# Splitting 45 of the second layer's weights ahead of time into memory, and moving one PSUM bank from dense to small products

## The chip, the cores and the metric

The kernel runs on one core of a Trainium2 chip. The metric is the device time of one execution in microseconds (us), the median of three runs for the kernel before. TensorE is called PE below, VectorE DVE, ScalarE ACT, GpSimd POOL, and SyncE, which here does nothing but issue the DMAs, SP.

## The reference, cut to what matters

Two layers over 512 positions of width 1024, float32, and a final norm:

```
h = x + even_layer(rms_norm(x, g0), w_in (1024 x 7168), ..., w_out (2048 x 1024))
h = h + odd_layer(rms_norm(h, g1), w_in (1024 x 5248), ..., w_out (1536 x 1024))
out = rms_norm(h, final_norm_g)

even_layer: p = h @ w_in, split in 7; a gated width-3 convolution and a gated
            128x128 position mixing; concat @ w_out
odd_layer:  p = h @ w_in, split in r, k, v, two low-rank streams, gate zc, fd, zd;
            RWKV-7 scans forward and backward, 16 heads of 64; a 2-D DFT branch on fd;
            SiLU gates; concat @ w_out
```

## The kernel before, in words

**Dense products.** A weight is cut into pieces of 128x1024 (512 KB): 8 (`pv`), 48 (`ub`, `zb`, `xa`, `ca`, `za`, `ba`) and 16 (`e0_*`, `e1_*`, the output projection) in the first layer, 41 input blocks (`wa`, `k`, `r`, `v`, `zc`, `fd`, `zd`) and 12 output pieces (`o0_*`, `o1_*`) in the second. PE multiplies in float32r, so each piece is split first: hi = the piece copied to float32r, lo = piece - hi, and likewise the activations; a product is the three matmuls hi*hi, hi*lo, lo*hi (`mm3`). One input block is 24 matmuls of 512 columns into one PSUM bank. So a weight costs one DMA (`loads`, tile `wf_...` of ring `wq`), one cast (`copy`: ACT, or DVE where the planner finds that sooner) and one subtraction (`less`: POOL or DVE, likewise) in `splits`.

**Small products.** The scans are cut into chunks of 64 positions. For each of 8 pairs of heads j there are many small float32 matmuls: scores (`sm`, `sa`, `sz`), a 64x64 triangular inverse by blocks (`iH`, `iTT`, `iTB`, `iG`, `iTJ`, with a long row of small DVE operations `iA`, `iT` ahead of it), `sp`, `sg`, and the chain over 8 chunks (`pa`, `py`, DVE's `X`). Each result in PSUM goes to SBUF by a DVE or ACT operation before its bank is free.

**Order.** Every part is a generator, a *strand* with a rank. `Plan.run` builds the program in one pass: it picks, time after time, the operation that could start first by the planner's own table of costs (lower rank first among equals) and appends it to its engine's queue. The engines then run these queues in order. A tile is taken from a ring of fixed size (`get`) and given back (`free`); a strand that finds no free tile waits. Rings that matter here: `wq` (5 tiles of 512 KB), `kb` (2), `a` (2), `zg` (3) of 256 KB; and the PSUM rings `d` (3 banks: dense blocks, the low-rank products `zw`, `za`, and `bo`) and `s` (3 banks: the small products, most of which ask for two banks at once), `py`, `pa` (1 each). At most 3 weights are loaded and not yet split (`credit`).

Of the kernel before, what the change touches and what calls it, by code (L numbers as in the profile page):

```python
# [12 lines left out]
F32 = mybir.dt.float32  # L13
# [11 lines left out]
C = 64  # L25
# [392 lines left out]
OUTS = 0, 1, 2, 4, 5, 3  # L418
LAST = 1, 2
FLAGS = False, False, False  # L420


class Slabs:
# [9 lines left out]
class K:  # L433
# [42 lines left out]
    def turned(self, x, s, h, g, key, ss):  # L476
# [14 lines left out]
        self.free("zg", t)  # L491
        self.plan.done.add(f"{key}{s}_{h}")

    def loads(self):
        yield "go"
        for i, (key, src, shape) in enumerate(self.weights):
            if key == "wa0":
                for _ in range(2):
                    yield from self.plan.credit("load", 3)
            yield from self.plan.credit("load", 3)  # L500
            wf = self.wf[key] = yield from self.get("wq", f"wf_{key}", shape)
            yield self.Q.dma_start(wf, src)
            self.plan.done.add(f"wf_{key}")

    def splits(self):

        layer0 = True
        for i, (key, src, shape) in enumerate(self.weights):
            layer0 = layer0 and key != "wa0"
            yield f"wf_{key}"  # L510
            if key == "pv1_0":
# [2 lines left out]
            if key.startswith("pv") and key.endswith("_0"):  # L514
                at = []
                for tag in ("G", "ops"):
                    at.append((tag, (yield from self.get(tag, f"w{tag}_{key}", shape, F32R))))
                tiles = [t for _, t in at]
            elif key in (f"o0_{OUTS[-1]}", f"o1_{OUTS[-2]}"):
                at = []  # L520
                for n in "hl":
                    at.append(("xw", (yield from self.get("xw", f"w{n}_{key}", dt=F32R))))
                tiles = [t for _, t in at]
            elif key in ("e1_5", "e1_6"):
                tag, low = ("wq", "k") if key == "e1_5" else ("E", "r")
                t = yield from self.get(tag, f"w_{key}", shape, F32R)
                at = [(tag, t)]
                for _ in range(2):
                    at.append((low, (yield from self.get(low, f"w_{key}", [P, 1, 512], F32R))))
                tiles, parts = [t, Slabs(at[1][1], at[2][1])], [slice(0, 1), slice(1, 2)]  # L530
            elif key == "e1_7":
                at = []
                for tag in ("a", "a", "w", "w"):
                    at.append((tag, (yield from self.get(tag, f"w_{key}", [P, 1, 512], F32R))))
                tiles, parts = [Slabs(at[0][1], at[1][1]), Slabs(at[2][1], at[3][1])], [slice(0, 1), slice(1, 2)]
            else:
                low = "hi" if key == "k0" else "wq" if not layer0 else "xw" if key[0] in "puz" and key[:2] != "za" else ("hi", "E")[i % 2]
                tiles, at = [], []
                for tag in ("wq", low):
                    t = yield from self.get(tag, f"w_{key}", shape, F32R)  # L540
                    tiles.append(t)
                    at.append((tag, t))
# [22 lines left out]
    def project(self, name, n, y, res, pair):  # L565

        for d in range(2):
            ps, tags = [None] * NS, (("d", "d", "d", "py"), ("s", "s", "s", "d"))[d]
            for bs in [(b,) for b in range(n - 3)] + ([(n - 3, n - 2, n - 1)] if d == 1 and pair else [(n - 3,), (n - 2,), (n - 1,)]):
                for b in bs:  # L570
                    yield f"w_{name}{d}_{b}"
# [970 lines left out]
    def project_o(self, d):  # L1542
# [5 lines left out]
        else:  # L1548
            self.gb = yield from self.get("vq", "fin_gb", [P, D])
            yield self.Q.dma_start(self.gb, self.I["fin_g"].to_broadcast([P, D]))  # L1550
        ps, tags = [None] * NS, (("d", "d", "d", "s"), ("pa", "s", "s", "py"))[d]
        def part(b, s):
            w = self.w[f"o{d}_{b}"][0]
            if ps[s] is None:
# [82 lines left out]
    def run(self):  # L1637
        I = self.I
        with ExitStack() as ctx:
# [2 lines left out]
            self.tp = tp = self.pool(ctx, "work")  # L1642
            self.ip = self.pool(ctx, "scan")
            dram = self.pool(ctx, "dram", 1, bass.MemoryType.DRAM)
            dp, sp, yp, cp = (self.pool(ctx, name, n, PSUM) for name, n in (("dense", 3), ("short", 3), ("outs", 1), ("chain", 1)))
            self.h1 = dram.tile([S, D], F32, name="h1_dram")
            self.yd = dram.tile([6, P, S], F32, name="y_dram")
            fz = dram.tile([8, P, S], F32, name="f_dram")
# [13 lines left out]
                self.ring(tag, shape, 1, self.ip)  # L1662
            self.ring("X", [P, 4, 64], 2, self.ip)
            self.ring("wq", [P, KB, P], 5, self.wp)
            self.ring("d", [P, S], 3, dp)
            self.ring("s", [P, 8, C], 3, sp)
            self.ring("py", [P, S], 1, yp)
            self.ring("pa", [P, 4, 64], 1, cp)
            self.blocks = [("wa", 0), ("k", 0)] + list(FIRST)
# [15 lines left out]
            at = {"wa": 24, "k": 8, "r": 0, "v": 16, "zc": 25, "fd": 33, "zd": 37}  # L1685
            self.weights += [(f"{b}{j}", I["w_o"][at[b] + j], [P, KB, P]) for b, j in self.blocks]
            self.weights += [(f"o{d}_{b}", I["w_oo"][d, b], [P, 2, 512]) for d in range(2) for b in OUTS]
            self.w, self.wf, self.out, self.g = {}, {}, {}, [{"j": j} for j in range(8)]
            self.yh0, self.yl0, self.fss, self.h2 = {}, {}, {}, [None] * NS
            self.pool_r, self.pool_k, self.pool_t = FLAGS  # L1690
            for rank, gen in ((0, self.chain()), (1, self.start()), (1, self.build()), (3, self.post()), (4, self.loads()), (4, self.splits()), (4, self.prep()),
                              (5, self.products()), (6, self.params1()), (6, self.unit_states()), (FR, self.fnet()), (6, self.reload())):
                plan.strand(rank, gen, rank == 0, rank == 5)
            plan.run()
# [26 lines left out]
```

## Time and profile before

| what | value |
|---|---|
| median of 3 runs | 1087.21 us (1084.24 to 1088.44) |
| profiled execution | 1090.07 us, span 1088.3 us |
| instructions in the span | 27301 |
| busy: PE, DVE, ACT, POOL | 94%, 60%, 43%, 11% |
| DMA | 91.51 MB, 84 GB/s over the span |
| granted PE clock, mean | 0.983 |

"Busy" counts the time in which an engine had at least one instruction running; PE's matmuls are pipelined and their records overlap. The span goes from the first to the last instruction. All operations are recorded in one place, line 401, so tiles, not lines, tell what an instruction is; buffer numbers are left out of names.

### The profile page before, as it was taken

To read this page: it belongs to the slowest core of one execution; us is meant where nothing else is said; L and a number is where in the kernel's file an instruction comes from. 1 tells how busy PE (TensorE), PEld (TensorE's weight loads), DVE (VectorE), ACT (ScalarE), POOL (GpSimd) and SP (SyncE) were. 2 spreads that over 40 slices of the span, in tenths; PEclk is the share of its full clock that TensorE was granted. 3 is DMA by queue.
4 is the path that set the end of the run, shared out by engine and by line. 5 is a ranking of instruction groups with operands and counts; after the bars stand their busy time and mean duration, and the time that the engine had idled before them with its cause. 6 is when DMAs were issued, how large, how long until landed. Compare 5 with 4: busy or idle time off the path is not lost. (4 is left out here: it accounts for less than half of the span.)

```text
span 1088.3 us, 27301 instructions
## 1 busy us (share of the span) xinstructions
PE 1024.3 (94%) x12024; PEld 839.3 (77%) x12024; DVE 651.3 (60%) x1225; ACT 472.7 (43%) x795; POOL 124.9 (11%) x155
## 2 busy tenths in 40 slices
PE   7999999999999999998898999989988899999997
PEld 6988888888888888876676778767767677777776
DVE  6464444344343336895795858867793976864453
ACT  7232222222222125753565455744644736453253
POOL 1001210010110010220012101321021201110000
PEclk9999999999999999999998999989998999999999
DMA  8322222322223332332012011110121111154033
GB/s 286 105 73 94 81 94 98 97 97 97 96 96 124 130 116 98 100 105 89 8 46 89 3 42 61 49 52 21 41 71 41 60 39 48 60 172 131 30 107 117
DMA packets 32663, 91.51 MB, mean 84 GB/s; under 512 B 4896, under 2 KB 7712, under 8 KB 32544
## 3 DMA queue, kind: packets, MB, share of 16 engines
q1 hardware_dynamic: 32544, 89.77, 25.1%
q8 instruction: 94, 1.54, 0.6%
q14 instruction: 25, 0.20, 0.1%
HBM read 81.82 MB, written 7.86 MB: 82 GB/s over the span
## 5 line engine op out<-in xcount | busy, mean ns | idle before, releaser
L401 PE MATMUL pe<-w_e,yh 128*128 128x512 f32 x256 | 81.5, 398 | 0.0
L401 PE MATMUL sg<-ops 64*128 64x128 f32 x512 | 66.6, 294 | 7.2 <-ACT am L401 2.1
L401 PEld LDWEIGHTS sg<-ops 64*128 64x128 f32 x512 | 53.9, 196 | 17.1 <-issue 3.9
L401 PE MATMUL sg<-pt,am 64*128 64x128 f32 x512 | 60.5, 283 | 0.0
L401 PEld LDWEIGHTS pe<-w_e,yh 128*128 128x128 f32 x256 | 48.1, 188 | 11.6
L401 ACT COPY gq<-sg 128x256 f32<-128x256 f32 x64 | 23.2, 370 | 71.7 <-DVE gq L401 70.5
L401 PEld LDWEIGHTS sg<-pt,am 64*128 64x128 f32 x512 | 52.3, 195 | 0.0
L401 PE MATMUL pd_zc<-hh,w_zc 128*128 128x512 f32 x128 | 50.5, 437 | 1.3 <-DVE w_zc L401 1.3
L401 PE MATMUL pe<-w_e,yl 128*128 128x512 f32 x128 | 50.3, 393 | 0.0
L401 DVE TENSOR_TENSOR w_e<-wf_e,w_e 128x1024 fp32r<-128x1024 f32 (+1 forms) x19 | 20.0, 1074 | 48.0 <-ACT w_e L401 47.8
L401 PE MATMUL pd_r<-hh,w_r 128*128 128x512 f32 x128 | 45.5, 409 | 2.0 <-DVE w_r L401 2.0
L401 DVE TENSOR_TENSOR gq<-sg,c_masks 128x256 f32<-128x256 f32 x64 | 25.6, 416 | 33.7 <-PE sg L401 33.7
L401 PE MATMUL pd_k<-hh,w_k 128*128 128x512 f32 (+1 forms) x144 | 44.6, 372 | 0.0
L401 PEld LDWEIGHTS pa<-X,gq 128*64 128x64 f32 x448 | 30.8, 139 | 17.1 <-issue 3.9
L401 ACT CAST w_e<-wf_e 128x1024 fp32r<-128x1024 f32 (+1 forms) x19 | 16.9, 913 | 62.4 <-PE pe L401 54.6
L401 PE MATMUL pd_v<-hh,w_v 128*128 128x512 f32 x128 | 43.8, 410 | 0.0
L401 PE MATMUL pa<-X,gq 128*64 128x64 f32 x448 | 38.8, 230 | 4.6 <-DVE X L401 2.0
L401 PE MATMUL pa<-c_cen,vq 128*64 128x128 f32 x256 | 42.6, 288 | 0.0
L401 PE MATMUL pd_ub<-hh,w_ub 128*128 128x512 f32 x128 | 40.5, 393 | 0.0
L401 PE MATMUL pd_zb<-hh,w_zb 128*128 128x512 f32 x128 | 40.4, 392 | 0.0
L401 PE MATMUL pd_xa<-hh,w_xa 128*128 128x512 f32 x128 | 40.4, 392 | 0.0
L401 PE MATMUL pd_ca<-hh,w_ca 128*128 128x512 f32 x128 | 40.4, 392 | 0.0
(362 smaller groups left out, 2831.4 us busy)
## 6 DMA issues: line engine op xcount, KB each, us to landing
wf_e<-in_w_eo SPq DMA_DIRECT2D x16, 512.0 KB
wf_o<-in_w_oo SPq DMA_DIRECT2D x12, 512.0 KB
wf_pv<-in_w_ev SPq DMA_DIRECT2D x8, 512.0 KB
wf_ub<-in_w_e SPq DMA_DIRECT2D x8, 512.0 KB
wf_zb<-in_w_e SPq DMA_DIRECT2D x8, 512.0 KB
wf_xa<-in_w_e SPq DMA_DIRECT2D x8, 512.0 KB
wf_ca<-in_w_e SPq DMA_DIRECT2D x8, 512.0 KB
wf_za<-in_w_e SPq DMA_DIRECT2D x8, 512.0 KB
```

The source lines that it names most:

```text
L401: i = op.call(*op.a, **op.kw)
```

## The change

Two edits, both in the code that makes the order. (1) A new strand of the lowest rank, `stash`, runs once the first norm is done. For the last 45 of the 53 weights of the second layer (33 input blocks, all 12 output pieces) it loads each in two halves of 256 KB, casts (`sh`), subtracts (`sl`; on POOL unless DVE would be done 4.0 us sooner by the planner's costs) and writes both results to a tensor in device memory, `w_dram`. `loads` then brings such a weight as two DMAs of 512 KB, hi and lo (`wh_...`, `wl_...`), and `splits` handles the other 80 alone. (2) The PSUM ring `d` has 2 banks in place of 3, `s` 4 in place of 3; three lists of tags follow.

```diff
+EARLY, STASH = 8, 4.0
+    def stash(self):
+        yield "consts"
+        yield "n0_3"
+        for n, (key, src, shape) in enumerate(self.late):
+            w = self.ws[key] = self.wd[n]
+            for i in range(2):
+                c = slice(4 * i, 4 * i + 4) if shape[1] == KB else slice(i, i + 1)
+                x = yield from self.get("zg", f"sf_{key}{i}")
+                yield self.Q.dma_start(x.rearrange("p (a b) -> p a b", b=shape[2]), src[:, c])
+                self.plan.done.add(f"sf{2 * n + i}")
+                self.plan.strand(7, self.apart0(2 * n + i, key, x, [w[h, :, i * S:i * S + S] for h in range(2)]))
+    def apart0(self, n, key, x, to):
...
+        hi = yield from self.get("kb", f"sh{n}", dt=F32R)
+        yield self.copy(hi, x)
+        lo = yield from self.get("a", f"sl{n}", dt=F32R)
+        yield self.less(lo, x, hi, STASH)
+        self.free("zg", x)
...
+        yield self.Q.dma_start(to[0], hi[:].bitcast(F32))
+        self.free("kb", hi)
+        yield self.Q.dma_start(to[1], lo[:].bitcast(F32))
+        self.free("a", lo)
     def loads(self):
...
+            if key in late:
...
+                for h in range(2):
+                    t = yield from self.get(tag, f"w{'hl'[h]}_{key}", shape, F32R)
+                    yield self.Q.dma_start(t[:].bitcast(F32).rearrange("p a b -> p (a b)"), self.ws[key][h])
     def project(self, name, n, y, res, pair):
-            ps, tags = [None] * NS, (("d", "d", "d", "py"), ("s", "s", "s", "d"))[d]
+            ps, tags = [None] * NS, (("d", "s", "s", "py"), ("s", "s", "d", "s"))[d]
     def project_o(self, d):
-        ps, tags = [None] * NS, (("d", "d", "d", "s"), ("pa", "s", "s", "py"))[d]
+        ps, tags = [None] * NS, (("d", "d", "s", "s"), ("pa", "s", "s", "py"))[d]
     def run(self):
-            dp, sp, yp, cp = (self.pool(ctx, name, n, PSUM) for name, n in (("dense", 3), ("short", 3), ("outs", 1), ("chain", 1)))
+            dp, sp, yp, cp = (self.pool(ctx, name, n, PSUM) for name, n in (("dense", 2), ("short", 4), ("outs", 1), ("chain", 1)))
-            self.ring("d", [P, S], 3, dp)
-            self.ring("s", [P, 8, C], 3, sp)
+            self.ring("d", [P, S], 2, dp)
+            self.ring("s", [P, 8, C], 4, sp)
+            self.late, self.ws = self.weights[-(len(self.blocks) - EARLY + 12):], {}
+            self.wd = dram.tile([len(self.late), 2, P, 1024], F32, name="w_dram")
```

Since the planner places everything anew, the order changes on all engines. On SP's queue, in the first layer's blocks, before the change there are only the weights of these blocks:

```order
L401 DMA wf_xa_1832<-in_w_e 128x1024
L401 DMA wf_xa_1868<-in_w_e 128x1024
L401 DMA wf_ca_1902<-in_w_e 128x1024
L401 DMA wf_ca_1937<-in_w_e 128x1024
L401 DMA wf_za_1971<-in_w_e 128x1024
L401 DMA wf_za_2006<-in_w_e 128x1024
```

On the same queue in the changed kernel, at the first `xa` weights (`sf` a half that is loaded, `sh` and `sl` its parts):

```order
L401 DMA wf_xa_1538<-in_w_e 128x1024
L401 DMA w_dram<-sh_1504 128x512
L401 DMA w_dram<-sl_1514 128x512
L401 DMA sf_r_1560<-in_w_o 128x512
L401 DMA w_dram<-sh_1532 128x512
L401 DMA w_dram<-sl_1543 128x512
L401 DMA sf_r_1582<-in_w_o 128x512
L401 DMA wf_xa_1599<-in_w_e 128x1024
L401 DMA sf_zd_1608<-in_w_o 128x512
L401 DMA w_dram<-sh_1566 128x512
L401 DMA w_dram<-sl_1575 128x512
```

Between two weights of the first layer there now stand five to six DMAs of 256 KB, two of three of them writes that wait for ACT's or POOL's result. All 270 of them (90 loads, 180 writes) stand between the sixth `pv` weight and the first `e` weight.

On PE's queue in the second layer, at the last chunks of the chain of the sixth pair of heads, before the change a dense block (`pd_zc`) and the product `bo` stand between two steps of the chain (`pa`, `py`):

```order
L401 MATMUL pa<-X_5_6556,gq_10_6484 64x64
L401 MATMUL py_6331<-gq_10_6484,X_5_6556 64x64 x4
L401 MATMUL bo_0_6572<-hi_0_6573,ones_193 128x512 x2
L401 MATMUL pd_zc_6206<-hh,w_zc_6193 128x512
L401 MATMUL pd_zc_6206<-hl,w_zc_6193 128x512
L401 MATMUL pd_zc_6206<-hh,w_zc_6194 128x512
```

At the same place on PE's queue of the changed kernel there are small products alone:

```order
L401 MATMUL pa<-X_5_7313,gq_10_7253 64x64
L401 MATMUL py_7125<-gq_10_7253,X_5_7313 64x64 x4
L401 MATMUL sz_10_7361<-ops_3931 64x128
L401 MATMUL sz_10_7361<-ops_3934 64x128
L401 MATMUL sz_11_7362<-ops_3931 64x128
L401 MATMUL sz_11_7362<-ops_3934 64x128
```

The dense blocks have moved together: the longest row of small products without a dense one between is 170 instructions before and 286 after, with the same matmuls in all.

## Rows read from the trace of the kernel before

**Rows 1.** The page: engines' busy time, and the span in 40 slices.

```profile
PE 1024.3 (94%) x12024; PEld 839.3 (77%) x12024; DVE 651.3 (60%) x1225; ACT 472.7 (43%) x795; POOL 124.9 (11%) x155
...
PE   7999999999999999998898999989988899999997
...
DVE  6464444344343336895795858867793976864453
```

**Rows 2.** Busy time by stage: stretch, length, engines busy, PEclk, DMA share, GB/s.

```profile
25.00:313.00 288.00, 288.00 (x1441) 244.09 (x1440) 132.00 (x177) 80.25 (x105) 26.14 (x23) 1.00 0.28 92
313.00:434.00 121.00, 121.00 (x572) 99.75 (x571) 47.11 (x62) 37.45 (x52) 10.49 (x13) 1.00 0.35 118
434.00:1043.00 609.00, 559.07 (x9744) 448.25 (x9743) 436.29 (x925) 320.75 (x575) 84.79 (x112) 0.97 0.19 62
```

**Rows 3.** Who waited for whom, PE alone, 434 to 1043 us.

```profile
PE iTT L401 <- DVE iHs L401: 7.5, 3, 3.3
PE iTB L401 <- issue: 3.3, 2, 2.2
PE iH L401 <- issue: 3.3, 2, 2.1
...
PE pd_r L401 <- DVE w_r L401: 2.0, 1, 2.0
...
PE pd_zc L401 <- DVE w_zc L401: 1.3, 2, 0.9
```

**Rows 4.** The chain that ended last: first and last of its six pieces on splits.

```profile
859.92 1.13 DVE w_k L401
...
1032.66 1.22 DVE w_o L401
```

**Rows 5.** Groups by shape from 400 us on: splits on DVE, ACT and POOL.

```profile
L401 DVE TENSOR_TENSOR w_k<-wf_k,w_k 128x1024 fp32r<-128x1024 f32 x8 | 9.8, 1226 | 0.6 <-ACT w_k L401 0.4 <-issue 0.2
...
L401 DVE CAST w_v<-wf_v 128x1024 fp32r<-128x1024 f32 x1 | 1.7, 1725 | 0.0
...
L401 DVE CAST w_k<-wf_k 128x1024 fp32r<-128x1024 f32 x1 | 0.7, 684 | 0.0
...
L401 ACT CAST w_k<-wf_k 128x1024 fp32r<-128x1024 f32 x7 | 7.3, 1049 | 3.6 <-DMA wf_k<-in_w_o 3.6
...
L401 ACT CAST w_e<-wf_e 128x512 fp32r<-128x512 f32 x6 | 3.2, 618 | 4.6 <-PE pe L401 4.6
...
L401 POOL TENSOR_TENSOR w_v<-wf_v,w_v 128x1024 fp32r<-128x1024 f32 x4 | 9.7, 2436 | 62.7 <-ACT w_v L401 40.5 <-PE pd_fd L401 14.5 <-PE iH L401 7.7
```

**Rows 6.** DMA share and rate (last two columns) in three short stretches.

```profile
5.00:10.00 5.00, 2.94 (x13) 2.47 (x14) 2.32 (x6) 4.71 (x10) 0.00 (x0) 1.00 1.01 391
10.00:15.00 5.00, 4.55 (x19) 3.67 (x17) 5.00 (x10) 5.00 (x10) 0.00 (x0) 1.00 1.06 367
966.00:970.00 4.00, 4.00 (x23) 3.30 (x21) 0.91 (x3) 3.34 (x4) 0.00 (x0) 1.00 0.94 293
```

**Rows 7.** SP's queue in order of time, first and last of six transfers of 256 KB.

```profile
963.42 0.94 SPq L401 DMA_DIRECT2D yf<-y_dram  x1
...
966.30 0.43 SPq L401 DMA_DIRECT2D xr<-h_dram  x1
```

**Rows 8.** Same, then ACT: a 512 KB load with nothing beside it.

```profile
402.57 0.33 SPq L401 DMA_DIRECT2D wf_wa<-in_w_o  x1
...
406.42 1.05 ACT L401 CAST w_wa<-wf_wa 128x1024 fp32r<-128x1024 f32 x1 [2.87 <-DMA wf_wa<-in_w_o]
```

**Rows 9.** SP and ACT in order of time: loads of two blocks, their casts.

```profile
86.82 6.77 SPq L401 DMA_DIRECT2D wf_ub<-in_w_e  x2
...
101.87 1.05 ACT L401 CAST w_ub<-wf_ub 128x1024 fp32r<-128x1024 f32 x1 [4.39 <-PE pd_zb L401]
```

**Rows 10.** By tile, PE: count, duration ns min/median/max, first and last start.

```profile
L401 PE MATMUL pd_ub<-hh,w_ub x128: 387/392/476, 61.5 to 143.8; 128*128 128x512 f32 x128
...
L401 PE MATMUL pe<-w_e,yh x256: 386/398/478, 332.6 to 423.7; 128*128 128x512 f32 x128
```

More of the change, by code (lines that the diff above doesn't have):

```diff
@@ L492, in turned @@
         self.plan.done.add(f"{key}{s}_{h}")
+    def stash(self):
[10 more added lines that the diff above has]
+    def apart0(self, n, key, x, to):
+        if n + 1 < 2 * len(self.late):
+            yield f"sf{n + 1}"
+        if n:
+            yield f"sl{n - 1}"
+        hi = yield from self.get("kb", f"sh{n}", dt=F32R)
+        yield self.copy(hi, x)
+        self.plan.done.add(f"sh{n}")
+        lo = yield from self.get("a", f"sl{n}", dt=F32R)
+        yield self.less(lo, x, hi, STASH)
+        self.free("zg", x)
+        self.plan.done.add(f"sl{n}")
+        if n + 1 < 2 * len(self.late):
+            yield f"sh{n + 1}"
+        yield self.Q.dma_start(to[0], hi[:].bitcast(F32))
+        self.free("kb", hi)
+        yield self.Q.dma_start(to[1], lo[:].bitcast(F32))
+        self.free("a", lo)
+        self.plan.done.add(f"st{n}_")
     def loads(self):
         yield "go"
+        late = {key for key, _, _ in self.late}
         for i, (key, src, shape) in enumerate(self.weights):
+            if key in late:
+                if key == self.late[0][0]:
+                    yield f"w_{self.weights[i - 1][0]}"
+                n = 2 * [k for k, _, _ in self.late].index(key)
+                yield f"st{n}_"
+                yield f"st{n + 1}_"
+                tag, at = "xw" if key in (f"o0_{OUTS[-1]}", f"o1_{OUTS[-2]}") else "wq", []
+                for h in range(2):
+                    t = yield from self.get(tag, f"w{'hl'[h]}_{key}", shape, F32R)
+                    yield self.Q.dma_start(t[:].bitcast(F32).rearrange("p a b -> p (a b)"), self.ws[key][h])
+                    at.append((tag, t))
+                self.w[key] = [t for _, t in at], at
+                self.plan.done.add(f"w_{key}")
+                continue
             if key == "wa0":
@@ L507, in splits @@
         layer0 = True
-        for i, (key, src, shape) in enumerate(self.weights):
+        for i, (key, src, shape) in enumerate(self.weights[:len(self.weights) - len(self.late)]):
             layer0 = layer0 and key != "wa0"
@@ L517, in splits @@
                     at.append((tag, (yield from self.get(tag, f"w{tag}_{key}", shape, F32R))))
[L518 to L522, printed above, removed]
                 tiles = [t for _, t in at]
@@ L1690, in run @@
             self.pool_r, self.pool_k, self.pool_t = FLAGS
-            for rank, gen in ((0, self.chain()), (1, self.start()), (1, self.build()), (3, self.post()), (4, self.loads()), (4, self.splits()), (4, self.prep()),
+            for rank, gen in ((0, self.chain()), (1, self.start()), (1, self.build()), (3, self.post()), (4, self.loads()), (4, self.splits()), (7, self.stash()), (4, self.prep()),
                               (5, self.products()), (6, self.params1()), (6, self.unit_states()), (FR, self.fnet()), (6, self.reload())):
```

## The prediction, made before the changed kernel was run

> **What bounds the kernel now.** I read the page first, then busy time by stage, then PE's waits, then the chain, then the DMA rows. The page shows PE busy 94% of the span, DVE 60%, and by slices two different halves: PE is full from the second slice to the seventeenth, while DVE stands at three or four tenths; after that PE loses a tenth in most slices and DVE stands at seven to nine [rows 1]. The stages say it in us. From 25 to 313 us (the first layer's blocks) PE is busy all 288 us, DVE 132, ACT 80, POOL 26, and the DMA engines 0.28 of their time. From 434 to 1043 us (the second layer up to the end of its small products) PE is busy 559 of 609 us, so 49.9 us are idle, with DVE at 436 (72%) and ACT at 321 (53%) [rows 2]. So the first layer is bound by PE alone, and its other engines have room. The second is PE too, but with 50 us of waits, and the most that any change to the other engines can give there is those 50 us and what the clock takes: a mean of 0.97 is 0.03 x 609 x 2 = 37 us at the lower level.
>
> Who ends these waits? By PE's own list about 9 us are "issue" (its instruction stream, which no other engine shortens; the two largest are 3.3 each), 2.0 + 1.3 = 3.3 us are a dense block waiting for DVE's subtraction for its weight, and some 36 us are small products waiting for DVE or ACT, the largest the inverse (`iTT`, 7.5) [rows 3]. The chain that ended last, which the trace follows back to 860 us, runs in turn over DVE and PE and has six pieces that are splits, 7.28 us in all (1.13, 1.05, 1.62, 1.21, 1.05, 1.22) out of 228 [rows 4].
>
> **What the change does, part by part.**
>
> *Second layer, splits gone.* Of the splits of the second layer the order shows 48 fewer on DVE (41 subtractions, 7 casts), 38 fewer casts on ACT, 4 fewer subtractions on POOL. At 1.226 us a subtraction and about 0.95 a cast (eight on DVE, from 0.684 to 1.725), DVE loses 50.3 + 6.7 = 57 us, and ACT 38 x 1.049 = 40 us [rows 5]. That is 13% of DVE's work in this stage and 12% of ACT's. What PE gets of it: the 3.3 us of direct waits go (a weight can now be late only by its DMA). Of the other 36 us, between nothing (each wait is a dependency that stands anyway) and all. I take a quarter, twice the share of the work that goes, since an in-order queue at 72% makes more than its share of lateness: 9 us. A check from the chain: 7.28 us in 228, taken over 654 us from 434 to the end, would be 21 us if nothing else became late in their place. My 12.3 us lies between the direct waits and that.
>
> *Second layer, DMA.* 45 weights cost two DMAs in place of one: 23.6 MB more over 609 us, 39 GB/s beside the 62 that are there at a share of 0.19. That is hidden. Its cover is the ring: two tiles for the block that runs, two for the next, one over. A load with nothing beside it took 3.85 us from issue to use [rows 8] and a block on PE lasts 5.65 us (48 blocks of 24 matmuls from 61.5 to 332.6 us [rows 10]), so it comes in time. If it were uncovered, each block would wait up to 3.85 us; I take nothing.
>
> *PSUM.* The fourth small bank lets the next pair of banks fill while the last is emptied; the second edit of the order shows what it costs: with two dense banks `pd`, `zw`, `za` and `bo` queue for the same two, dense blocks stand together, and small products run 286 instructions on end where it was 170. Where small products stand alone, PE can hide no wait. Both go into the quarter above; their bounds are 0 and the 36 us on one side, and on the other side a rival below. The clock I leave as it is: both signs are possible, with 37 us at the lower level to win from.
>
> *First layer, splits added.* 90 casts of 128x512: 86 on ACT by the order, at 0.618 us 53 us in 288 where ACT is busy 80; 90 subtractions on POOL at half of 2.436 us, 110 us where POOL is busy 26 [rows 2, 5]. Both fit. POOL and DVE can hold each other up (a DVE cast that takes 0.684 us elsewhere took 1.725 once [rows 5]): at worst 90 times 1.04 us, 94 us on a DVE with 156 us free. Cover enough; what would be late without it is emptying a dense bank, of which there are now two, one per 5.65 us of matmuls. The three tag lists give the output projections as many banks as before from other rings; PE is busy 121 of 121 us there [rows 2], and I take nothing.
>
> *First layer, DMA: the term that can turn the sign.* Between 25 and 313 us SP now issues 90 loads and 180 writes of 256 KB, 70.8 MB, beside 50 weights of 512 KB, 26.2 MB. 97.0 MB in 288 us is 337 GB/s, where it was 92 [rows 2]. What can the DMA engines do? With 512 KB loads queued they moved 391 and 367 GB/s at a share of 1.01 and 1.06 [rows 6]. With six transfers of 256 KB issued within 3.3 us [rows 7] the stretch 966 to 970 shows 293 GB/s at 0.94, so 312 at a full share [rows 6]. Mixed by bytes, with 379 as the mean of the first two, 70.8/312 + 26.2/379 = 227 + 69 = 296 us, 8 us more than there are. Slack: a weight was issued at 86.82 us and cast at 101.87, when ACT waited for PE and not for the load [rows 9]; less the 3.85 us of a load, 11 us of delay cost nothing. So the middle estimate costs 0, the lower rate as it stands (97.0/293 = 331 us, 43 - 11) costs 32, the higher rates cost 0. SP itself has time (320 issues at about 0.4 us in 288 us), but it waits in order: behind a write that waits for POOL stand the next weights of the first layer, and PE waits for those. I take 3 us for that.
>
> **Sum.** Against the profiled execution, 1090.07 us: -3.3 - 9 + 3 = -9.3 us, 1080.8 us. The runs' median is 2.9 us below that execution, so 1077.9; I say 1078 us, 0.85% faster.
>
> **The rivals.**
>
> *The first layer becomes bound by its DMAs (slower).* For it: 337 GB/s wanted, 293 to 312 seen with transfers of this size, and writes beside reads on queues that wait for two engines. Against it: 367 to 391 seen with a deep queue, and the order gives the weights a lead. At 293 GB/s: +32 - 12.3 = +20, 1107 us. The point from which it decides: it costs nothing down to 97.0/299 = 324 GB/s, and eats the whole gain of 12.3 us at 97.0/311 = 312.
>
> *The pieces do not overlap.* If every transfer paid its own latency in turn, as the lone load did (3.85 us for 512 KB [rows 8]; 0.69 less for 256 KB at 379 GB/s), 270 x 3.16 + 50 x 3.85 = 1046 us would stand in place of 288, and the whole would be some 1820 us. The six that were issued in 3.3 us and moved at 293 GB/s [rows 6, 7] speak against it. The Trainium skill, SBUF — State Buffer, section on the DMA setup-cost knee, measured 224 GB/s for single transfers of 256 KiB; by that the stage would be 97.0/224 = 433 us, an estimate of some 1210 us in all. The 293 GB/s of this trace is above that, because here several transfers were queued.
>
> *PE's waits only change their owner (no change).* With 94% busy and 9 us of issue, the inverse's row of DVE operations still stands ahead of `iTT`; the direct 3.3 us go and SP's 3 us come: 1087 us.
>
> *All of it is won.* The 36 us, the 3.3 and nothing lost: 1087.2 - 39 = 1048 us; for it speaks DVE's part in the chain, against it that waits on dependencies remain.
>
> *Dense blocks run out as cover.* If the longer rows of small products open new waits of 1 to 3 us at each of the eight pairs of heads, 8 to 24 us come back; with none of the quarter won, about 1100 us.
>
> **How the numbers follow.** This kernel's runs differ by 0.4%, so a change under 0.5% (5.4 us) can't be told from none. Forecast (a gain of 6 to 25 us): 0.40. All won or nearly: 0.12. Together faster 0.52. No change: 0.20. Slower: DMA-bound 0.20, dense cover 0.06, pieces that don't overlap 0.02, together 0.28. The likeliest case's own range is 1062 to 1081. The range of 8 in 10 runs from 1055 (it leaves out some 0.08 of "all won") to 1110 (it leaves out the pieces that don't overlap and DMA rates under 293, some 0.08).
>
> **What would show each step.** Right, if PE is still busy all through the blocks, the first `pe` matmul stays near 333 us, and the DMA share in the blocks is 0.85 to 0.98; wrong, if PE shows waits for `w_ub`, `w_xa` and their like and the first `pe` comes 10 us or more later: the DMA rival. In the second layer DVE's busy time should be down by some 50 us and PE's idle time in it from 50 us to about 38; if DVE is down and PE's idle time is not, the waits have changed owner; if new waits of `sg`, `sp`, `sa` for `gq`, `am`, `zz` come up inside long rows of small products, it is the dense cover. Waits of `pd` matmuls for DMAs of `wh` or `wl` would show that the reload is not hidden. The prediction fails most easily on the DMA rate with writes among reads, which no row of before shows at this load.

## The result, and the profile after

The changed kernel takes 1159.39 us, median of 4 runs (1158.99 to 1171.45), beside 1087.71 us of the kernel before (1084.24 to 1088.44, 4 runs): ratio 1.068, 95% interval 1.065 to 1.072, so 6.8% slower. The prediction said 1078 us, 1055 to 1110. The profiled execution took 1159.49 us where that of before took 1090.07: 69.4 us more, and three places of the trace say where. The page, busy time and the slices (PE, granted clock, DMA share, GB/s), answers to [rows 1]:

```profile
PE 1050.3 (91%) x12024; PEld 848.5 (73%) x12024; DVE 617.6 (53%) x1182; ACT 482.8 (42%) x842; POOL 234.9 (20%) x241
...
PE   7969888988798799999989999899998898999997
...
PEclk9979998999899899999999999999999999999999
DMA  8777778888787742332430232213150403335344
GB/s 299 262 238 250 234 263 275 264 284 273 235 262 248 261 128 91 129 126 93 154 139 8 96 123 84 80 56 114 43 168 9 156 8 115 116 130 176 117 155 163
```

The tiles `pe` and `pd_ub` (as [rows 10]) say when the first layer's blocks end and how long one matmul takes, the windows (as [rows 2], cut at the first `pe` and the first `pd_wa`, the start of the second layer) what the engines did:

```profile
L401 PE MATMUL pe<-w_e,yh x256: 387/398/477, 420.9 to 512.0; 128*128 128x512 f32 x128
...
L401 PE MATMUL pd_ub<-hh,w_ub x128: 387/394/793, 67.4 to 180.1; 128*128 128x512 f32 x128
```

```profile
25.00:421.00 396.00, 343.03 (x1524) 272.93 (x1523) 162.78 (x190) 129.46 (x195) 150.93 (x117) 0.93 0.76 251
421.00:512.00 91.00, 91.00 (x400) 73.33 (x399) 34.04 (x44) 26.71 (x36) 3.68 (x6) 1.00 0.37 125
512.00:1157.00 645.00, 598.76 (x9995) 486.18 (x9993) 404.76 (x919) 309.17 (x581) 78.53 (x112) 0.98 0.31 104
```

First layer: the first `pe` comes at 420.9 us in place of 332.6, 88.3 us late. Of these PE is idle 53 (396 less 343.0), and its 343 busy us hold the work that took 308 before (25 to 332.6): the other 35. The granted clock was 0.93 in place of 1.00, because in some stretches the lower of the two levels was granted (a `pd_ub` matmul takes up to 793 ns there, where 476 was the most before [rows 10]). That accounts for at most 0.07 x 396 = 28 of the 35 us; the rest was not followed. Output projection: 91.5 us as before. Second layer: from `pd_wa` to the end 645.3 us where it was 664.1, 18.8 us won. 88.3 - 18.8 - 0.1 = 69.4.

PE's own waits, first layer (top five) and second layer (top three, to set against [rows 3]):

```profile
PE pd_ub L401 <- DVE w_ub L401: 12.0, 4, 5.4
PE pd_ba L401 <- DVE w_ba L401: 6.7, 3, 3.1
PE pd_ca L401 <- ACT w_ca L401: 6.7, 3, 3.8
PE pv L401 <- ACT x L401: 4.2, 2, 4.0
PE pd_ba L401 <- ACT za L401: 3.9, 3, 1.6
...
PE iTB L401 <- issue: 6.8, 2, 3.5
PE sm L401 <- issue: 4.1, 4, 1.7
PE iH L401 <- issue: 3.6, 3, 2.0
```

In the first layer PE waits mostly for the splits of that layer's own weights (40 us by the whole list); the other 12 are dense banks that are emptied late (`x`, `za` and their like). Neither is ACT or DVE short of time (129 and 163 us busy of 396). What they and POOL wait for stands in the list of all engines for 25 to 421 us, and then in SP's:

```profile
ACT sh L401 <- DMA w_dram<-sh: 164.8, 61, 10.7
POOL sl L401 <- DMA w_dram<-sl: 80.6, 21, 6.3
POOL sl L401 <- ACT sh L401: 69.5, 24, 7.5
...
SPq L401 <- POOL sl L401: 167.5, 80, 4.9
```

ACT stands 165 us before casts of the stash, because by the profile the tile for the result is still being written out; behind that cast in ACT's queue stands `w_ca`, for which PE waits. SP stands 168 us for POOL's subtractions. The rows in order of time show how these close a ring (SP, then ACT, then POOL):

```profile
205.26 0.33 SPq L401 DMA_DIRECT2D sf_zc<-in_w_o  x1
205.65 0.42 SPq L401 DMA_DIRECT2D w_dram<-sh  x1
206.12 0.42 SPq L401 DMA_DIRECT2D w_dram<-sl  x1
207.77 0.33 SPq L401 DMA_DIRECT2D sf_k<-in_w_o  x1
208.15 0.44 SPq L401 DMA_DIRECT2D w_dram<-sh  x1
...
211.79 0.33 SPq L401 DMA_DIRECT2D sf_k<-in_w_o  x1
...
209.79 0.62 ACT L401 CAST sh<-sf_zc 128x512 fp32r<-128x512 f32 x1 [0.84 <-DMA w_dram<-sh]
...
212.26 0.62 ACT L401 CAST sh<-sf_zc 128x512 fp32r<-128x512 f32 x1 [0.42 <-DMA w_dram<-sh]
...
206.46 1.29 POOL L401 TENSOR_TENSOR sl<-sf_v,sh 128x512 fp32r<-128x512 f32 x1
210.49 1.27 POOL L401 TENSOR_TENSOR sl<-sf_zc,sh 128x512 fp32r<-128x512 f32 x1 [2.74 <-ACT sh L401]
```

The load at 207.77 goes out the moment a subtraction ends (206.46 + 1.29) and frees its source tile. The write at 205.65 lands, and 4.14 us after its issue the cast two pieces later can start (209.79); for the next write 4.11 (208.15 to 212.26). The subtraction follows (210.49 to 211.76), and at 211.79 SP's next load. Over all pieces the median from a write's issue to the cast that it holds up is 4.29 us, and a piece takes 4.15 us (first to last of 90 subtractions). The order has less room. At the last stash load, 387.9 us, PE had 33 us of blocks left; at full speed that load would stand 33 us before 332.6, so 90 loads lie between 21.4 and 300 us: 3.1 us each. Fixed orders turn the difference into a toll on PE: about 1 us for each of 90 pieces.

### The profile page after: what moved, and what is told of

Same layout as the page of the kernel before. It is cut to its first block, busy times and chain, and to the rows that moved or that the text cites. A ratio compares the mean times of both kernels' runs of the same rounds, so it can differ in the third digit from the quotient of the medians.

```text
span 1157.7 us, 27995 instructions
## 1 busy us (share of the span) xinstructions
PE 1050.3 (91%) x12024; PEld 848.5 (73%) x12024; DVE 617.6 (53%) x1182; ACT 482.8 (42%) x842; POOL 234.9 (20%) x241
## 4 chain that ended last, share of the span: by engine, by line
PE 50%; DVE 10%; issue 3%; ACT 3%; DMA 1%; SPq 0%; POOL 0%; DVEq 0%; ACTq 0%
PE pe L401 8%; PE po L401 6%; PE pd_zc L401 4%; PE pd_v L401 4%; PE sg L401 4%; PE pd_r L401 3%; PE pd_k L401 3%; DVE iA L401 2%; PE pd_fd L401 2%; PE pa L401 2%; DVE iT L401 2%; PE pd_zd L401 1%; PE sp L401 1%; DVE gq L401 1%; PE sm L401 1%
## 5 line engine op out<-in xcount | busy, mean ns | idle before, releaser
L401 PE MATMUL sg<-ops 64*128 64x128 f32 x512 | 61.9, 285 | 2.3 <-ACT pt L401 1.3
L401 PE MATMUL pd_ub<-hh,w_ub 128*128 128x512 f32 x128 | 46.2, 439 | 15.9 <-DVE w_ub L401 12.0
L401 PEld LDWEIGHTS sg<-ops 64*128 64x128 f32 x512 | 49.8, 187 | 9.0 <-ACT pt L401 2.9
L401 PE MATMUL pd_ba<-hh,w_ba 128*128 128x512 f32 x128 | 45.4, 430 | 10.8 <-DVE w_ba L401 6.7
L401 PE MATMUL pd_ca<-hh,w_ca 128*128 128x512 f32 x128 | 44.5, 424 | 8.3 <-ACT w_ca L401 6.7
L401 PE MATMUL pd_za<-hh,w_za 128*128 128x512 f32 x128 | 41.6, 400 | 5.3 <-DVE w_za L401 2.9
L401 POOL TENSOR_TENSOR sl<-sf_o,sh 128x512 fp32r<-128x512 f32 x24 | 33.0, 1379 | 64.0 <-ACT sh L401 22.8
L401 ACT CAST sh<-sf_o 128x512 fp32r<-128x512 f32 x23 | 14.3, 622 | 74.0 <-DMA w_dram<-sh 50.2
L401 PEld LDWEIGHTS pd_ub<-hh,w_ub 128*128 128x128 f32 x128 | 26.8, 213 | 25.0 <-DVE w_ub L401 14.2
L401 PE MATMUL pd_xa<-hh,w_xa 128*128 128x512 f32 x128 | 42.3, 406 | 2.4 <-ACT w_xa L401 1.5
L401 PEld LDWEIGHTS pd_ba<-hh,w_ba 128*128 128x128 f32 x128 | 25.9, 206 | 21.2 <-DVE w_ba L401 9.4
```

The lines of the kernel that those rows point to most:

```text
L401: i = op.call(*op.a, **op.kw)
```

## The experiments

"First `pe`" is 332.6 us before and 420.9 after; the period is from the first to the last subtraction of the stash over the number between; rate and share are those of the window from 125 to 325 us; the second layer is from the first `pd_wa` to the end of the span.

| run | ratio (95% interval) | period us | first `pe` us | GB/s, share | second layer us |
|---|---|---|---|---|---|
| before | 1 | - | 332.6 | - | 664.1 |
| changed kernel | 1.068 (1.065-1.072) | 4.15 | 420.9 | 262, 0.79 | 645.3 |
| banks alone | 1.005 (1.003-1.007) | - | 332.0 | - | 665.6 |
| stash alone | 1.076 (1.072-1.081) | 4.12 | 419.6 | 262, 0.80 | 662.7 |
| 30 weights | 1.061 (1.058-1.065) | 4.16 | 390.7 | 224, 0.69 | 674.9 |
| four tiles | 1.050 (1.047-1.054) | 4.00 | 403.3 | 262, 0.79 | 643.4 |
| reads for writes | - | 4.33 | 428.3 | 251, 0.78 | - |
| small writes | - | 3.23 | 382.4 | 177, 0.61 | - |
| paced, 24 weights | 0.996 (0.993-0.998) | 5.90 | 331.9 | 232, 0.73 | 654.5 |
| POOL's queue | 1.049 (1.043-1.054) | 4.20 | 392.4 | 267, 0.81 | 648.4 |
| more in flight | 1.066 (1.061-1.071) | 4.15 | 417.6 | 259, 0.79 | 653.7 |
| paced, 32 weights | 1.011 (1.008-1.013) | 5.84 | 333.5 | 236, 0.74 | 672.2 |
| low parts | 0.994 (0.992-0.996) | 4.12 | 332.6 | 226, 0.68 | 657.6 |
| paced 24, old banks | 1.008 (1.006-1.011) | 5.90 | 332.3 | 232, 0.72 | 670.4 |
| free writes | - | 3.15 | 338.4 | 333, 0.96 | - |
| paced, 45 weights | 1.041 (1.038-1.045) | 5.14 | 333.2 | 270, 0.83 | 673.2 |
| POOL's queue, four tiles | 1.009 (1.006-1.011) | 3.40 | 356.8 | 330, 0.94 | 651.0 |
| writes first, four tiles | 0.995 (0.993-0.996) | 3.35 | 341.2 | 338, 0.99 | 651.5 |
| writes first, two tiles | 1.026 (1.024-1.028) | 3.66 | 374.9 | 296, 0.89 | 647.7 |
| writes first, paced | 1.019 (1.014-1.023) | 4.64 | 341.4 | 312, 0.92 | 675.1 |

**Which edit.** Banks alone (the rings, pools and tag lists of the diff, on the kernel before):

> The PSUM edit alone, no weights kept. If the stash alone explains the loss, the first layer keeps its place: the first `pe` matmul within 2 us of the 332.6 us of before, where the changed kernel has 420.9. For the second layer (664.1 us from `pd_wa` to the end before, 645.3 after) there are two theories. If the 18.8 us won there come from the splits that went, this run has 660 to 675 us there and 1083 to 1099 in all; if they come from the fourth small bank, it has 645 to 652 us and 1068 to 1076 in all.

Stash alone (the changed kernel with three and three banks):

> The weights kept in memory, with three dense and three small banks as before. If the lost time in the first layer comes from the stash and not from the two dense banks (a late evacuation of a bank would then stop PE), the first `pe` matmul comes at 415 to 425 us as in the changed kernel; if the two banks share the blame, it comes before 405. The second layer: 640 to 652 us if the splits that went give the gain, 655 to 665 if the banks do. In all 1150 to 1170 by the first, under 1145 by the second.

The loss is the stash's alone: 332.0 and 419.6 us. The gain came only with both edits: the second layer is as before with either (665.6, 662.7 against 664.1) and 18.8 us shorter with both, which neither expectation had.

**A toll on each piece, or too many bytes in all.** `EARLY = 23` keeps 30 weights:

> 30 of the 45 weights are kept, 60 pieces in place of 90; the other 15 are split in the second layer. If the loss is a toll on each piece, because SP, ACT and POOL take pieces and first-layer weights in one fixed order and a piece takes some 4.2 us where the order has room for 3.2 (88 us for 90 pieces, 1 us each), the first `pe` matmul comes at 333 + 59 = 392 us, and the total is about 1130. If the DMA engines are simply asked for more than they carry over the whole stage (26.2 + 47.2 = 73.4 MB at the 258 GB/s that the changed kernel moved is 285 us, which fits in the 288), it comes at 333 to 345 us and the total is about 1075 to 1090.

390.7 us, as the toll says: 58.1 us for 60 pieces, 0.97 each, as 88.3 for 90 is 0.98.

**More tiles.** Four tiles for each part, `hi` in turn from `kb` and `at`, `lo` from `a` and `bon`, and then also five source tiles, in turn from `zg` and `y`:

```diff
+        th, tl = ("kb", "at")[n % 2], ("a", "bon")[n % 2 if n > 11 else 0]
```

> The changed kernel with four tiles in place of two for each of the two parts of a piece (a second ring of two is taken in turn, idle in the first layer), so that a tile may wait for its write twice as long. If a piece's time is set by latency (a tile of the part is held some 4.3 us from the issue of its write until it lands, and there are two), pieces follow each other in 3.2 us or less and the first `pe` matmul comes at 335 to 360 us, the total at 1075 to 1100. If the DMA engines' rate with reads and writes mixed is the limit (97 MB at 258 GB/s is 376 us), nothing comes of it: the rate stays at 250 to 270 GB/s, the first `pe` matmul at 405 to 425 us, the total at 1145 to 1165.

> The run with four tiles for each part, and from the thirteenth piece on five source tiles in place of three (the two of a ring that is idle then), so that 13 tiles instead of 7 can have a transfer under way. In the run with four tiles a source tile was held 12.0 us (7.2 from issue to cast, the rest cast, wait and subtraction), three times the 4.0 us between pieces. If the number of tiles in flight sets the rate, pieces now follow in 3.0 to 3.4 us, the rate goes over 300 GB/s and the first `pe` matmul comes at 340 to 375 us. If the DMA engines and SP's queue set it, more in flight only waits longer: the load takes 9 us or more to its cast, the rate stays at 255 to 280 GB/s and the first `pe` matmul at 390 to 415 us.

Both came out on the side of the DMA engines' rate: 262 and 259 GB/s. But that reading, mine for a while, is wrong. In the run with 13 tiles, SP's rows and POOL's show bursts and not a steady load:

```profile
207.91 0.33 SPq L401 DMA_DIRECT2D sf_zc<-in_w_o  x1
208.34 0.38 SPq L401 DMA_DIRECT2D wf_za<-in_w_e  x1
208.77 0.42 SPq L401 DMA_DIRECT2D sf_k<-in_w_o  x1
209.25 0.42 SPq L401 DMA_DIRECT2D w_dram<-sl  x1
...
211.10 0.52 SPq L401 DMA_DIRECT2D w_dram<-sh  x1
215.92 0.33 SPq L401 DMA_DIRECT2D sf_k<-in_w_o  x1
...
206.60 1.29 POOL L401 TENSOR_TENSOR sl<-sf_zd,sh 128x512 fp32r<-128x512 f32 x1 [4.54 <-issue]
...
214.60 1.29 POOL L401 TENSOR_TENSOR sl<-sf_v,sh 128x512 fp32r<-128x512 f32 x1 [5.33 <-DMA w_dram<-sl]
```

Seven transfers leave in 3.7 us, then SP stands from 211.62 to 215.92 for the subtraction at 214.60, which waits 5.33 us for a tile whose write went out in the same burst. The order had used the new tiles to put the writes later (a median of 8.8 us after the subtraction, 1.7 in the changed kernel), so they came free no sooner.

**Bytes, direction, waits.** Reads of the same size in place of the writes, from the third piece on (all three edits stand at `apart0`'s two writes; `hi`'s is shown; `to[2]` is the piece's place in the weight):

```diff
+        yield self.Q.dma_start(to[0], hi[:].bitcast(F32)) if n < 2 else self.Q.dma_start(hi[:].bitcast(F32).rearrange("p (a b) -> p a b", a=to[2].shape[1]), to[2])
```

> The changed kernel with each write of a part (178 of 180) replaced by a read of the same 256 KB into the same tile, in the same queue; the second layer reloads the first kept weight in place of all, so only the first layer is to be read. If the rate of 250 to 262 GB/s is that of writes mixed with reads, reads alone go at 300 GB/s or more and the first `pe` matmul comes at 335 to 375 us. If it is the rate of 256 KB transfers as such, or the wait for each tile to land, nothing changes: 410 to 425 us at 250 to 265 GB/s.

An eighth of each write, `m = 64` of 512 columns from the third piece on:

```diff
+        yield self.Q.dma_start(to[0][:, 0:m], hi[:, 0:m].bitcast(F32))
```

> The changed kernel with 64 of 512 columns in each write of a part (178 of 180), an eighth of the bytes, in the same number of issues; the second layer reloads the first kept weight in place of all, so only the first layer is to be read. If bytes are the limit (26.2 + 23.6 + 5.9 = 56 MB in place of 97; at 258 GB/s 216 us), the toll goes: the first `pe` matmul at 333 to 345 us. If it is the order of SP's queue with its waits for ACT and POOL, whatever the bytes, it comes at 395 to 425 us. If it is the time until a write has landed, it is in between, 345 to 380.

Writes of a finished tensor, `self.h`, in place of `hi` and `lo`:

```diff
-        yield self.Q.dma_start(to[0], hi[:].bitcast(F32))
+        yield self.Q.dma_start(to[0], self.h[0][:, n % 8].bitcast(F32))
```

> The changed kernel with the writes taken from the finished halves of the layer's input (128x512, the same 256 KB) in place of the parts just made, so that a write waits for neither ACT nor POOL, and a part's tile is free once the subtraction is done; bytes, number and place of the transfers stay. What is reloaded in the second layer is not the weights, so only the first layer is to be read. If the loop of waits sets the 4.15 us, pieces follow in 3.2 to 3.5 us, the rate is 300 GB/s or more and the first `pe` matmul comes at 333 to 360 us. If the DMA engines' rate sets it, the rate stays at 255 to 280 GB/s, a piece at 3.9 to 4.2 us and the first `pe` matmul at 395 to 420.

Reads are no better (428.3 us), so writing as such is not the matter. With 56 MB in place of 97, 50 us are still lost, at a share of 0.61. (The order of this run leaves a piece less room besides: its last stash load stands 73 us before the first `pe`, so at full speed 90 loads have 2.6 us each, and a piece took 3.23.) And with all 97 MB, but writes that wait for neither ACT nor POOL and hold no part's tile, the toll is 5.8 us. Windows of the changed kernel, of this run, and of the one with writes first:

```profile
125.00:325.00 200.00, 173.04 (x694) 133.51 (x693) 78.06 (x79) 65.67 (x96) 81.23 (x59) 0.93 0.79 262
```

```profile
125.00:325.00 200.00, 200.00 (x892) 164.65 (x891) 112.95 (x106) 80.45 (x114) 107.61 (x70) 1.00 0.96 333
```

```profile
125.00:325.00 200.00, 200.00 (x892) 164.52 (x891) 103.11 (x104) 83.57 (x118) 105.10 (x73) 1.00 0.99 338
```

The DMA engines carry the stash at 333 to 338 GB/s, half of it writes; 262 was what the ring of waits asked of them.

**Which link of the ring.** The load of piece m only after the write of piece m - 3 is issued, with two tiles and with four:

```diff
+                if 2 * n + i > 2:
+                    yield f"st{2 * n + i - 3}_"
                 x = yield from self.get("zg", f"sf_{key}{i}")
```

> The same order of loads and writes with the two tiles of the changed kernel for each part. From its cast to the landing of its write a tile is held some 0.6 + 2.0 (wait and subtraction) + 4.3 = 7 us, so two tiles allow a piece in 3.5 us. If the place of the writes is all that matters, as good as the run with four, 333 to 352 us at the first `pe`; if the tiles matter too, 350 to 375; if only the tiles and their landing matter, 400 to 421 as in the changed kernel.

> The run with four tiles, and the load of a piece released only by the write of the piece three before it, so that SP's queue holds one load and two writes in turn and no write stands behind a load that waits for a later subtraction. If the place of the writes in the queue closes the loop, pieces follow in 3.1 to 3.4 us, the rate is 310 GB/s or more and the first `pe` matmul comes at 333 to 352 us; with the second layer of the changed kernel (737 us from there) 1070 to 1090 in all. If it is the landing of the writes with the POOL and ACT waits in any order, it stays at 3.9 us or more and 390 to 410 us.

Late by 88.3 us (two tiles, old order), 70.7 (four tiles), 42.3 (writes first), 8.6 (both): relieving one link alone leaves 42 to 71 us, both together open the ring. SP's rows with both show one load and two writes in turn, 0.6 us (median) from the end of a subtraction to its write:

```profile
208.32 0.33 SPq L401 DMA_DIRECT2D wf_ca<-in_w_e  x1
208.70 0.42 SPq L401 DMA_DIRECT2D w_dram<-sh  x1
209.22 0.38 SPq L401 DMA_DIRECT2D w_dram<-sl  x1
209.65 0.50 SPq L401 DMA_DIRECT2D sf_k<-in_w_o  x1
```

The stash on POOL's queue (`self.G.dma_start` in place of `self.Q.dma_start`), with two tiles and with four:

> The changed kernel with the stash's loads and writes issued by POOL on its own queue, the first layer's weights alone on SP's. If the loss is a head-of-line effect (weights wait in SP's order behind writes, and in the engines' queue behind the stash's bytes), the weights get through, the stash is done later, and the first `pe` matmul comes at 335 to 365 us. If the 16 engines' rate is shared whatever the queue, or ACT and POOL are held by tiles that wait for their writes, the first layer is as long as in the changed kernel, 400 us or more. The order also moves some 19 subtractions from POOL to DVE, 23 us of a DVE that is busy 0.4 there.

> The stash's loads and writes on POOL's queue as in the earlier run, and four tiles for each part. There a part's tile was free some 8 us after its cast (0.6 + 3.3 to the write's issue + 4.1 to its landing), two tiles, one piece in 4.2 us. If held tiles close the loop, four of them give room for a piece in 2 to 3 us, the period falls to 3.1 to 3.4 us and the first `pe` matmul comes at 335 to 355 us. If POOL itself is the limit there (a subtraction of 1.3 us and three issues, some 0.5 us each by its busy time, 2.9 us and its products for the first layer), the period is 3.4 to 3.8 and the first `pe` at 355 to 385 us.

59.8 us late, between the two cases expected, and 24.2: with four tiles the rate is there too (330 GB/s), and a piece takes the 3.4 us that were expected if POOL itself sets the pace (it is busy 158.6 of the 200 us). That the weights no longer stand behind waiting transfers is the likely reason for what was gained; 18 and 38 of the subtractions also went to DVE, so the queue is not tried by itself. The Trainium skill (DMA: Bandwidth & Descriptors, Issuing engines are not separate DMA queues) says that several issuing engines save only issue time; for the rate that agrees (330 here, 338 on SP alone). What these two runs saved, 28.5 and 46.5 us against the same tiles on SP's queue, is more than issue time, but what part of it is the queue's is not shown.

**Giving each piece more room.** A load waits for the issue of a further first-layer weight:

```diff
+                yield f"wf_{self.weights[8 + 2 * n + i][0]}"
```

With `EARLY = 29` (24 weights), the same with the old banks, and with `EARLY = 21` (32 weights):

> 24 weights kept, 48 pieces, and each piece's load released by the issue of one further first-layer weight, so one piece stands behind each weight over the whole stage: 0.52 + 0.79 = 1.31 MB per block of 5.65 us, 232 GB/s. If the toll is a rate that is asked for and can't be had (337 wanted, 258 given), it is gone here: the first `pe` matmul at 333 to 340 us. If each piece costs its 0.97 us wherever it stands, it comes at 333 + 47 = 380 us. For the second layer, 24 of 45 weights come ready: between the 664 us of before and the 645 us of the changed kernel if the gain follows the number of weights; the 675 us of the run with 30 speak against that. In all 1080 to 1100 without the toll.

> The paced run with 24 weights, with three dense and three small banks as before. The first layer as there, the first `pe` matmul at 331 to 335 us. With all 45 weights the second layer took 737 us from the first `pe` on with two dense banks and 754 with three, against 756 before. If the fourth small bank is needed for the gain, this run has 752 to 760 us there and 1085 to 1095 in all; if that difference was only how the order fell, 740 to 750 and 1072 to 1083.

> The paced run with 32 weights in place of 24: one piece behind each of the 64 weights from the ninth to the last of the first layer, so that 16 pieces fall into the output projection, where the DMA engines moved 118 GB/s before. The blocks should be as in the run with 24: the first `pe` matmul at 331 to 335 us. In the projection 0.52 + 0.79 = 1.31 MB per 7.6 us is 172 GB/s plus the residual's loads, so no toll: the first `pd_wa` at 423 to 426 us. If the gain of the second layer grows with the number of kept weights, it has 735 to 746 us from the first `pe` on (746 with 24, 737 with 45) and the total is 1068 to 1080; if it only depends on how the order falls, it is anywhere from 740 to 765 and the total 1073 to 1098.

All 45, by `weights[at[2 * n + i]]` with `at = [8 + n * 48 // 60 for n in range(60)] + [56 + n * 16 // 30 for n in range(30)]`; the low parts alone, paced over 64 weights, where `splits` loads `tiles[1]` from the kept tensor in place of `less`; and writes first, four tiles, by `weights[8 + (2 * n + i) * 56 // 90]`:

> All 45 weights kept, paced: 60 pieces behind the 48 weights of the blocks (1.25 per 5.65 us, so 4.52 us for each), 30 behind the 16 of the output projection (1.9 per 7.6 us, so 4.05 us for each). If the toll is the piece's 4.15 us less the room that the order gives it, the blocks pay nothing and the projection at most 0.1 x 30 = 3 us: the first `pe` matmul at 331 to 337 us, `pd_wa` at 423 to 430, and with the changed kernel's 645 us from there 1068 to 1076. If a rate of 0.52 + 1.25 x 0.79 = 1.51 MB per 5.65 us, 267 GB/s, can't be carried (258 was the most over long stretches), the blocks get (267/258 - 1) x 271 = 9 us longer and the projection likewise: `pd_wa` at 435 to 445, 1080 to 1090 in all.

> Only the low parts of the 45 weights are kept, paced over the 64 weights: 90 loads and 90 writes in place of 180 writes, 0.52 + 1.41 x 0.52 = 1.26 MB per block, 223 GB/s. The second layer loads a weight again, casts it for the high part as before and loads the low part in place of subtracting it. The first layer should pay no toll: the first `pe` matmul at 331 to 336 us. In the second layer DVE loses the 50 us of subtractions, ACT keeps the casts. If it is DVE's share that gave the 19 us, 735 to 748 us from the first `pe` on and 1068 to 1082 in all; if ACT's casts matter as much, 748 to 758 and 1082 to 1092.

> The run with four tiles and the writes ahead of the loads, and each load released besides by the issue of a first-layer weight: 90 pieces behind the 56 weights from the ninth to the middle of the output projection, 1.6 per block of 5.65 us, 0.52 + 1.6 x 0.79 = 1.78 MB, 316 GB/s where 339 were carried. If the last 8.6 us are the DMA engines' limit, the blocks now pay nothing, the first `pe` matmul comes at 331 to 335 us, and with 743 us from there as in that run the total is about 1073 to 1080. If a piece costs PE something whatever the rate, or the 10 to 13 pieces in the projection meet its own use of the same buffers (the paced run with all 45 lost 28 us there), the first `pe` or the first `pd_wa` is 5 us or more late and the total is 1080 to 1100.

Wherever the order left 4.5 us or more for a piece with a write of each part, the blocks paid under 1 us (331.9 to 333.5), so a piece costs PE nothing in itself; with one write for each piece the same held at 4.12 us (low parts). In the second layer the low parts won 6.5 us (657.6 for 664.1): that DVE is rid of its subtractions did not give the 18.8 by itself. The run with all 45 lost its time in the output projection, beside which 30 pieces stand: 129.0 us there in place of 91.6, with PE waiting 9.0 us for DVE's `w_e` and 6.9 for ACT's and a granted clock of 0.90. Pacing did not take away the last 8.6 us of the run with writes first: asked for 316 GB/s it was 8.8 late, most of it from one wait of 5.1 us,

```profile
PE pd_zb L401 <- DVE w_zb L401: 5.1, 1, 5.1
```

where the run without pacing has one too (`pd_ub` for `w_ub`, 4.6 us), with the lower clock after it. In the paced run the DMA engines are not what it waits for: their share was 0.36 and 0.37 (60 to 70 and 70 to 80 us), and both `w_zb` pieces had been cast by 74.2. Rows of DVE, then of POOL:

```profile
72.42 3.46 DVE L401 SCALAR_TENSOR_TENSOR x<-x,st,sgu_bb 128x512 f32<-128x512 f32 x2
75.81 1.84 DVE L401 SCALAR_TENSOR_TENSOR x<-x,st,sgu_gb 128x512 f32<-128x512 f32 x1
77.57 1.21 DVE L401 TENSOR_TENSOR w_zb<-wf_zb,w_zb 128x1024 fp32r<-128x1024 f32 x1
...
71.80 3.53 POOL L401 TENSOR_TENSOR sl<-sf_v,sh 128x512 fp32r<-128x512 f32 x2 [5.95 <-ACT sh L401]
75.84 1.26 POOL L401 TENSOR_TENSOR sl<-sf_zc,sh 128x512 fp32r<-128x512 f32 x1 [0.51 <-DMA w_dram<-sl]
```

The subtraction for `w_zb` stands in DVE's queue behind a norm of `x`, and three operations of this norm take 3.46 + 1.84 us while POOL subtracts for the stash. In the kernel before each of the 16 takes 0.75 us. By an estimate from these rows that is 3 of the 5.1 us; no run tries it. In the run without pacing `w_ub` stands behind the same norm, but at a DMA share of 0.91 (60 to 73.4 us), so the DMA engines may have a part in that wait.

The second layer's 670 to 675 us in five runs with some or all of the weights ready was not followed. Three have the stash reach into the projection, one has the old banks; the run with 30 has neither, so no one cause covers them. Mostly by this stretch the totals of the runs with 30 weights, with 32 and 45 paced, with the old banks and with writes first, paced, lie above what was expected of them (with all 45 by the projection too); stash alone lies 4 us above its range.

## Why the prediction was wrong

**The step that failed** is the last of the part on the first layer's DMAs: "it waits in order: behind a write that waits for POOL stand the next weights of the first layer ... I take 3 us for that". The mechanism was named; the term, put at 3 us, came to 88.3, with the lower clock that followed from the waits. I priced SP's wait once, and not as a ring. A write holds its tile for 4.3 us after issue; ACT and POOL stand for the tile, in front of the first layer's own casts; SP's next load stands for POOL, in front of that layer's weights. Rows of before could have warned of it. 90 pieces in the 288 us of the blocks are 3.2 us each. A cast of 0.62 us [rows 5], half of the 2.436 us subtraction [rows 5] and the 3.16 us worked out for 256 KB hold a tile for 5.0 us; with two tiles that is 2.5 us a piece, before any wait. So 0.7 us a piece was left for all waits in three in-order queues, and each 0.1 us beyond it costs 90 x 0.1 = 9 us: a wide range was the honest term, not 3. That it came to 1 us a piece only the runs showed.

**The DMA rate** was right. 337 GB/s wanted, "the higher rates cost 0": 333 to 338 were carried at a share of 0.96 and 0.99, above the 324 from which it was to cost nothing (these two runs were still 5.8 and 8.6 us late). The DMA rival's sign and place came true (PE waits for `w_ub` and its like, the first `pe` late), its cause did not: the share was 0.76 to 0.79 and the loss nearly three times its 32 us. By the curve of the Trainium skill (SBUF — State Buffer, The DMA setup-cost knee), which puts transfers of 256 KiB at 224 GB/s, the loss would have been more still. With several queued, this chip carried half as much again (338).

**Casts and subtractions** were as cheap as said, 0.62 and 1.30 us for one (groups by shape, first layer, to set against [rows 5]):

```profile
L401 POOL TENSOR_TENSOR sl<-sf_zc,sh 128x512 fp32r<-128x512 f32 x16 | 20.9, 1304 | 25.1 <-ACT sh L401 6.4 <-issue 4.8 <-DMA w_dram<-sl 4.6
...
L401 ACT CAST sh<-sf_zc 128x512 fp32r<-128x512 f32 x15 | 9.3, 622 | 31.2 <-DMA w_dram<-sh 30.3 <-POOL sl L401 0.9
```

What the prediction expected to be late without cover, "emptying a dense bank", made 12 us of PE's idle time and the first layer's own splits 40. Nor was the third bank the cure: with three (stash alone) PE waits for no bank there, and the loss is the same. That POOL and DVE "can hold each other up" was put at nothing as well ("Cover enough"); at the wait of 5.1 us above it shows, and there it is not covered.

**Second layer.** Forecast 12.3 us, measured 18.8: from `pd_wa` on PE's idle time fell by 9.5 (56.5 to 46.9) and its busy time by 9.3 (607.6 to 598.4). Of the latter the granted clock, that I had left as it was, makes only some 2.5 us (a mean of 0.972 and of 0.975); the rest was not followed. Inside the idle time the sizes were off both ways: by PE's list the waits for DVE and ACT fell from 39 to 19 us, by half and not by "a quarter", and "issue", which I took to stay at 9, rose to 20.6 (`iTB`, `sm` and `iH` above are its largest; what PE then waits for, the profile does not show). DVE lost 58 us (forecast 57), ACT 34 (40). The direct waits for subtractions are gone and no reload is waited for. That both edits went "into the quarter" hid that neither gives it alone. In the runs with all 45 weights and four small banks where the stash ended before the projection, it was 643 to 654 us, 10 to 21 us won. The 18.8 is near the top of these, and five other runs took 670 to 675: its size is in part luck of the order. With the term for the first layer near zero the forecast would have stood: free writes give 0.989 (0.984 to 0.994), though they reload something other than the weights; of the kernels with the whole computation, writes first with four tiles (1082.79 us), low parts (1083.24) and the paced 24 (1085.23) are 0.4 to 0.6% faster than before.

## What to carry to other kernels

When work is moved under another stage's cover, price the ring and not the engines: how long is each buffer held, from its first write until the transfer out has landed, divided by how many there are, against the room that the fixed order leaves for one item. Each in-order queue through which the item passes taxes everything behind it by the difference, however idle the engines are. A DMA share of 0.79 with flat rate is no proof of a limit; take the waits away and keep the bytes to see it, and more buffers help only if the order doesn't use them up by putting the release later.

## What the runs showed of the hardware that was not expected

256 KB transfers of 2 KB for each partition, a third of them loads and two thirds writes beside 512 KB loads, go at 338 GB/s over 200 us, more than the 293 that the trace of before showed at this size. In the kernel that was held by its waits, replacing the writes by reads made nothing faster (251 GB/s for 262). At a DMA share of 0.79 a write of 256 KB held its tile 4.1 to 4.3 us from issue; on POOL's queue it took 3.9 and 4.8 us (medians of `sh` and `sl`) to land at a share of 0.81, and 5.4 and 5.9 at 0.94. A DVE operation on `x` of 128x512 float32 took 0.75 us in the kernel before; in the run with writes first, paced, five of the seven that overlapped a POOL subtraction by 0.5 us or more took 1.7 to 2.9.
